# Rotary embedding from cached tables: the tables loaded into 64 partitions, with selections of 64 rows

## The chip, the cores and the metric

The kernel runs on one core of one Trainium2 chip. The metric is the time of one execution in microseconds (us). The profile's span is some 1.8 us shorter than that time, because it runs from the first to the last instruction of the program. A run that is more than 1.5% above the fastest of the same kernel counts as slow; slow runs are reported, but left out of the ratios.

## The reference

```python
# x: (8, 8, 1024, 64) float32; cos_cached, sin_cached: (1024, 32) float32
x_first, x_second = x[..., :32], x[..., 32:]
out_first  = x_first * cos_cached - x_second * sin_cached
out_second = x_first * sin_cached + x_second * cos_cached
```

Input and output are 16.8 MB each, each table is 128 KB.

## The kernel before

Eight tiles of x, 128 partitions of 16 KB each, are loaded, rotated and stored. A partition holds 64 successive positions of x, so that partition p needs the table rows of positions 64(p mod 16) to 64(p mod 16) + 63. The tables are loaded once, 8 positions to a partition, and TensorE spreads them: for each of eight blocks it multiplies the raw table by a selection matrix of zeros and ones, whose output row p picks the right raw row. A first product of the identity alone (`plus`) warms TensorE up.

```python
raw = sv[3][:, :BK]                              # 128 partitions, BK = 512
for eng, i, t in ((nc.sync, 0, sin_cached), (nc.scalar, 1, cos_cached)):
    eng.dma_start(out=raw[:, i * BK // 2:(i + 1) * BK // 2],
                  in_=t.rearrange("(q n) j -> q (n j)", q=P))
load(0, 0, F // 2); load(0, F // 2, F)           # x, all on SyncE's queue
# ... six more tiles; tile 7 in two pieces
sel = sv[3][:, BK:BK + N * P]                    # N = 2 * M = 8 selections side by side
nc.vector.tensor_copy(out=sel..., in_=plus...)   # built from the identity
nc.tensor.matmul(tp[6][:, :BK], plus, ...)       # warm-up
rt = raw.rearrange("q (t n j) -> q n t j", t=2, j=half)
for b, t in tp.items():                          # eight products in all
    for k in range(t.shape[1] // BK):
        nc.tensor.matmul(t[:, k * BK:(k + 1) * BK],
                         sel[:, (b + k) * P:(b + k + 1) * P], rt, start=True, stop=True)
# VectorE multiplies tile 0 straight from the products; ScalarE copies them to `tb` for the
# other tiles. VectorE, GpSimd and TensorE share the rest; all stores are on SyncE's queue,
# the first held back until the loads are nearly done.
```

(Before there are eight selections, in the change M = 4 that serve two products each.)

## Time and profile before

| | before |
|---|---|
| time, median (lowest to highest) | 85.07 us (85.02 to 85.08), 3 runs |
| span of the profile | 83.2 us |
| busy: VectorE, GpSimd, TensorE, ScalarE | 68.1, 65.2, 45.2, 38.1 us |
| moved by DMA | 33.8 MB, 407 GB/s over the whole span |
| last store issued / landed | 74.7 / 82.4 us |

The prediction shows the lines. PE is TensorE and PEld its weight loads, DVE is VectorE, ACT ScalarE, POOL GpSimd, SP SyncE; a q behind the name marks what the engine's queue does, such as issuing DMAs. A group in the profile reads: source line, engine, operation, output and input tile, shapes, count, then busy time, mean ns, and the idle time of the engine just before, with what ended it. An fp32 product appears as two TensorE records, which I call passes: eight products are 16 passes. The strips cut the span into 40 slices and give the busy share in tenths; PEclk is the share of TensorE's full clock that was granted, in tenths.

### The profile page before, as it was taken

The page shows a single profiled execution, that of the slowest core. Times are in us where ns is not written, and L with a number is a line of the kernel's source. Part 1 is how long each engine was busy: PE and PEld are TensorE (multiplying, and loading weights), DVE is VectorE, ACT ScalarE, POOL GpSimd, SP SyncE. Part 2 cuts the span into 40 slices and gives each one's busy share as a digit, 9 for nine tenths or more (in the row PEclk, how much of TensorE's full clock was granted, in tenths as well). Part 3 has the DMA queues.
Part 4 walks back from the last instruction along what each step waited for, and adds up shares of the span by engine and source line. Part 5 has one row for each costly group of instructions (what it writes and reads, how often), then busy time and mean ns, then how long its engine had stood idle before and what let it go on. Part 6 is the DMA issues. An engine that isn't in the chain of part 4 may idle for free.

```text
span 83.2 us, 393 instructions
## 1 busy us (share of the span) xinstructions
PE 45.2 (54%) x82; PEld 17.4 (21%) x82; DVE 68.1 (82%) x30; ACT 38.1 (46%) x34; POOL 65.2 (78%) x38
## 2 busy tenths in 40 slices
PE   3999960009971952994962948909959800000000
PEld 2244410004411401341411404204304200000000
DVE  3105999899999999999999999999999999980000
ACT  4322048954467627666449383694049290000000
POOL 3008998799999999999999999999999969920000
PEclk9999999855599999579999999996599999555555
DMA  1999999999999999989999999999999999999991
GB/s 20 346 402 445 465 402 449 433 410 457 410 465 402 418 457 402 465 377 423 428 434 465 418 410 457 402 473 402 418 465 402 457 402 473 410 410 402 420 426 44
DMA packets 3172, 33.82 MB, mean 407 GB/s; under 512 B 356, under 2 KB 612, under 8 KB 1124
## 3 DMA queue, kind: packets, MB, share of 16 engines
q1 hardware_dynamic: 3028, 33.69, 95.9%
q10 hardware_dynamic: 144, 0.13, 0.5%
HBM read 17.04 MB, written 16.78 MB: 407 GB/s over the span
## 4 chain that ended last, share of the span: by engine, by line
DVE 45%; DMA 25%; issue 12%; ACT 4%; SPq 3%; DVEq 1%
DVE w L117 40%; DMA w<-in_x_dram 25%; ACT st L124 4%; DVE st L117 3%; SPq L82 2%; DVE w L120 1%; DVEq L292 1%; SPq L77 0%; DVEq L117 0%; DVEq L120 0%
## 5 line engine op out<-in xcount | busy, mean ns | idle before, releaser
L117 DVE TENSOR_TENSOR w<-st,tb 128x3072 f32<-128x3072 f32 (+3 forms) x19 | 53.1, 2869 | 0.5 <-ACT st L124 0.5
L124 ACT COPY st<-w 128x1536 f32<-128x1536 f32 (+1 forms) x19 | 24.8, 1309 | 16.0 <-DVE w L117 16.0
L176 PE MATMUL acc<-w,plus 128*128 128x512 f32 x32 | 20.1, 714 | 19.6 <-ACT w L182 12.5
L120 POOL TENSOR_TENSOR w<-w 128x1024 f32<-128x1024 f32 (+4 forms) x12 | 25.0, 2086 | 1.9 <-DVE w L117 1.7
L121 POOL TENSOR_TENSOR w<-w 128x1024 f32<-128x1024 f32 (+4 forms) x12 | 25.0, 2085 | 0.0
L117 POOL TENSOR_TENSOR w<-w,tb 128x1280 f32<-128x1280 f32 (+1 forms) x6 | 14.2, 2368 | 5.5 <-DMA w<-in_x_dram 5.3
L176 PEld LDWEIGHTS acc<-w,plus 128*128 128x128 f32 x32 | 6.5, 224 | 31.7 <-ACT w L182 18.3
L117 DVE TENSOR_TENSOR w<-w,tab 128x2048 f32<-128x2048 f32 (+1 forms) x4 | 7.9, 2018 | 4.7 <-PE tab L227 4.7
L177 PE MATMUL acc<-w,minus 128*128 128x512 f32 x16 | 10.8, 768 | 0.0
L182 ACT COPY w<-acc 128x1024 f32<-128x1024 f32 x8 | 8.1, 1008 | 5.6 <-PE acc L177 5.6
L227 PE MATMUL tab<-w 128*128 128x512 f32 x16 | 8.2, 669 | 0.1
L177 PE MATMUL acc<-w,plus 128*128 128x512 f32 x16 | 8.2, 592 | 0.0
L235 ACT COPY tb<-tab 128x1024 f32<-128x1024 f32 (+1 forms) x5 | 4.2, 840 | 7.9 <-DVE w L117 5.0
L177 PEld LDWEIGHTS acc<-w,minus 128*128 128x128 f32 x16 | 3.8, 236 | 5.0 <-issue 5.0
L227 PEld LDWEIGHTS tab<-w 128*128 128x128 f32 x16 | 3.5, 223 | 5.6 <-issue 5.6
L177 PEld LDWEIGHTS acc<-w,plus 128*128 128x128 f32 x16 | 3.2, 199 | 4.4 <-issue 4.4
L117 DVE TENSOR_TENSOR st<-st,tb 128x1024 f32<-128x1024 f32 (+1 forms) x2 | 3.0, 1489 | 0.0
L222 PE MATMUL tab<-plus 128*128 128x512 f32 x2 | 2.1, 1140 | 1.4 <-POOL plus L100 1.4
L102 DVE COPY w<-plus 128x1024 f32<-128x1024 f32 x1 | 1.1, 1099 | 1.3 <-POOL plus L100 1.3
L105 ACT ACT_TABLE_LOAD x1 | 1.3, 1283 | 1.2 <-PEq L281 1.2
L120 DVE TENSOR_TENSOR w<-st,w 128x512 f32<-128x512 f32 (+1 forms) x2 | 1.6, 825 | 0.1
L121 DVE TENSOR_TENSOR w<-st,w 128x512 f32<-128x512 f32 (+1 forms) x2 | 1.6, 815 | 0.0
(10 smaller groups left out, 3.2 us busy)
## 6 DMA issues: line engine op xcount, KB each, us to landing
out_dram<-w SPq DMA_DIRECT2D x7, 2048.0 KB, 11.7
w<-in_x_dram SPq DMA_DIRECT2D x6, 2048.0 KB, 26.8
w<-in_x_dram SPq DMA_DIRECT2D x2, 1024.0 KB, 6.3
out_dram<-w SPq DMA_DIRECT2D x2, 768.0 KB, 7.7
w<-in_x_dram SPq DMA_DIRECT2D x1, 1280.0 KB, 34.3
w<-in_x_dram SPq DMA_DIRECT2D x1, 768.0 KB, 33.7
out_dram<-w SPq DMA_DIRECT2D x1, 512.0 KB, 7.1
w<-in_cos_cached_dram ACTq DMA_DIRECT2D x1, 128.0 KB, 2.8
```

The source lines that it names most:

```text
L82: return nc.sync.dma_start(out=xt[u][:, m0:m1], in_=xf[u][:, m0:m1])
L105: nc.scalar.mul(out=minus, in_=plus, mul=-1.0)
L117: eng.tensor_tensor(out=o, in0=a, in1=t, op=TT.mult)
L120: eng.tensor_tensor(out=o[:, :, 0], in0=c[:, :, 0], in1=s[:, :, 1], op=TT.subtract)
L121: eng.tensor_tensor(out=o[:, :, 1], in0=c[:, :, 1], in1=s[:, :, 0], op=TT.add)
L124: nc.scalar.copy(out=pt[:, :(n1 - n0) * hd], in_=xt[u][:, n0 * hd:n1 * hd])
L176: nc.tensor.matmul(a[:, k], plus, xr[:, :, k], start=True, stop=False)
L177: nc.tensor.matmul(a[:, k], plus if k else minus, sr[:, :, 1 - k], start=False, stop=True)
L182: nc.scalar.copy(out=rows(xt[u], n0, n0 + G), in_=a)
L222: nc.tensor.matmul(tp[6][:, :BK], plus, plus.unsqueeze(1).to_broadcast([P, BK // P, P]), start=True, stop=True)
L227: nc.tensor.matmul(t[:, k * BK:(k + 1) * BK], sel[:, (b + k) * P:(b + k + 1) * P], rt, start=True, stop=True)
L235: nc.scalar.copy(out=tb[:, b * BK:(b + n) * BK], in_=tp[b])
```

## The change

The intent is fewer and larger packets for the tables (2 KB rows, 64 of them, in place of 1 KB and 128) and a selection that costs half: 64 rows of four selections. Each selection serves two products, which read two halves of the raw rows.

```diff
+    Q = P // 2
-    raw = sv[3][:, :BK]
+    raw = sv[3][:Q, :2 * BK]
-        eng.dma_start(out=raw[:, i * BK // 2:(i + 1) * BK // 2],
-                      in_=t.rearrange("(q n) j -> q (n j)", q=P))
+        eng.dma_start(out=raw[:, i * BK:(i + 1) * BK],
+                      in_=t.rearrange("(q n) j -> q (n j)", q=Q))
...
+    M = N // 2
-    sel = sv[3][:, BK:BK + N * P]
+    sel = sv[3][:Q, 2 * BK:2 * BK + M * P]
-        in_=plus.rearrange("q (j k) -> q k j", k=N).unsqueeze(2).to_broadcast([P, N, N, S]))
+        in_=plus[:Q, :Q].rearrange("q (j k) -> q k j", k=M).unsqueeze(2)
+        .to_broadcast([Q, M, N, S]))
...
-    rt = raw.rearrange("q (t n j) -> q n t j", t=2, j=half)
+    rt = raw.rearrange("q (t h n j) -> q h n t j", t=2, h=2, j=half)
-                             sel[:, (b + k) * P:(b + k + 1) * P], rt,
+                             sel[:, (b + k) // 2 * P:((b + k) // 2 + 1) * P],
+                             rt[:, (b + k) % 2],
```

More of the change, by code (lines that the diff above doesn't have):

```diff
@@ L102 @@
     nc.vector.tensor_copy(
-        out=sel.rearrange("q (k r j) -> q k r j", k=N, j=S),
-        in_=plus.rearrange("q (j k) -> q k j", k=N).unsqueeze(2).to_broadcast([P, N, N, S]))
+        out=sel.rearrange("q (k r j) -> q k r j", k=M, j=S),
+        in_=plus[:Q, :Q].rearrange("q (j k) -> q k j", k=M).unsqueeze(2)
+        .to_broadcast([Q, M, N, S]))
     nc.scalar.mul(out=minus, in_=plus, mul=-1.0)
@@ L223 @@
                      start=True, stop=True)
-    rt = raw.rearrange("q (t n j) -> q n t j", t=2, j=half)
+    rt = raw.rearrange("q (t h n j) -> q h n t j", t=2, h=2, j=half)
     for b, t in tp.items():
         for k in range(t.shape[1] // BK):
-            nc.tensor.matmul(t[:, k * BK:(k + 1) * BK], sel[:, (b + k) * P:(b + k + 1) * P], rt,
-                             start=True, stop=True)
+            nc.tensor.matmul(t[:, k * BK:(k + 1) * BK], sel[:, (b + k) // 2 * P:((b + k) // 2 + 1) * P],
+                             rt[:, (b + k) % 2], start=True, stop=True)
     def first(b, n):
```

## The prediction

> **What bounds the kernel now.** I read the page's shares first, then the strips, then the queues, then the DMA issues, and last some stretches of time around the part that the change touches.
>
> ```profile
> span 83.2 us, 393 instructions
> PE 45.2 (54%) x82; PEld 17.4 (21%) x82; DVE 68.1 (82%) x30; ACT 38.1 (46%) x34; POOL 65.2 (78%) x38
> DVE  3105999899999999999999999999999999980000
> DMA  1999999999999999989999999999999999999991
> q1 hardware_dynamic: 3028, 33.69, 95.9%
> q10 hardware_dynamic: 144, 0.13, 0.5%
> ```
>
> VectorE (DVE) is the busiest engine with 68.1 us, but its strip ends four slices before the span does (a slice is 83.2/40 = 2.08 us), while the DMA strip is full from the second slice to the last but one. The two queues fill 96.4% of the time of the 16 DMA engines. The kernel moves 33.8 MB, and 33.69 MB in 0.959 x 83.2 = 79.8 us is 422 GB/s. So my reading is that the DMA engines bound it: they must start early, never run dry and be left with little extra to do. The chain of work that ended last says something else at first sight:
>
> ```profile
> DVE 45%; DMA 25%; issue 12%; ACT 4%; SPq 3%; DVEq 1%
> DVE w L117 40%; DMA w<-in_x_dram 25%; ACT st L124 4%; DVE st L117 3%; SPq L82 2%; DVE w L120 1%; DVEq L292 1%; SPq L77 0%; DVEq L117 0%; DVEq L120 0%
> ```
>
> That chain runs back from the last instruction of an engine, at 74 us, and does not contain the 8 us in which only stores drain. To see whether VectorE nonetheless holds the end, I ask how far ahead of the DMA engines the stores are issued:
>
> ```profile
> out_dram<-w SPq DMA_DIRECT2D x7, 2048.0 KB, 11.7
> out_dram<-w SPq DMA_DIRECT2D x2, 768.0 KB, 7.7
> out_dram<-w SPq DMA_DIRECT2D x1, 512.0 KB, 7.1
> w<-in_x_dram SPq DMA_DIRECT2D x2, 1024.0 KB, 6.3
> w<-in_cos_cached_dram ACTq DMA_DIRECT2D x1, 128.0 KB, 2.8
> w<-in_sin_cached_dram SPq DMA_DIRECT2D x1, 128.0 KB, 2.6
> ```
>
> A 2 MB store needs 2.10 MB / 430 GB/s = 4.9 us of its own and takes 11.7, so it stands behind some 6 us of other work and its receipt. The next view gives the slack of the last store: busy time of each engine by stretch, then the granted clock, the DMA share and the GB/s.
>
> ```profile
> 1.70:2.70 1.00, 1.00 (x2) 0.16 (x1) 0.74 (x1) 0.99 (x2) 0.00 (x0) 1.00 0.94 229
> 2.70:3.20 0.50, 0.50 (x1) 0.00 (x0) 0.00 (x0) 0.06 (x1) 0.00 (x0) 1.00 1.39 443
> 3.20:6.20 3.00, 2.85 (x5) 1.36 (x5) 0.00 (x0) 0.54 (x1) 0.00 (x0) 1.00 0.96 377
> ...
> 3.10:40.30 37.20, 24.30 (x44) 9.72 (x44) 32.85 (x13) 20.00 (x18) 32.39 (x17) 0.86 1.01 426
> ...
> 43.00:74.70 31.70, 16.50 (x32) 6.34 (x32) 31.43 (x16) 16.01 (x14) 29.42 (x14) 0.88 1.00 430
> ...
> 74.70:81.80 7.10, 0.00 (x0) 0.00 (x0) 0.00 (x0) 0.00 (x0) 0.00 (x0) 0.50 0.93 388
> ```
>
> The last store is issued at 74.7 us. After that the DMA engines still move 388 GB/s x 7.1 us = 2.75 MB, of which that store is 0.79 MB. So 1.97 MB were queued ahead of it, 4.6 us of work at 430 GB/s. VectorE could end some 4 us later, or any amount earlier, and the end would not move. The DMA share is 1.00 or 1.01 in both long stretches: there is no hole to fill. What is left to win or lose lies in the first three rows, where the tables and the first x packets go through: 229 GB/s in the first microsecond of traffic.
>
> **What the Trainium skill says.** Four places bear on it. "SBUF — State Buffer", section "Door 1: The DMA port swizzle (why [64,N] ≈ [32,N])": partitions 0 to 63 reach only 8 of the 16 ports through which DMA writes, and a 1 MiB transfer to 64 partitions measured 196 GB/s against 328 to 128. The kernel before has only 128-partition transfers, so its trace can neither confirm nor deny this. "DMA: Bandwidth & Descriptors", section "Why a DMA increments its semaphore by 16 and not by 1": a transfer whose slowest dimension is 64 is still split over 16 engines; every transfer of this trace lands in 16 parts, but those have 128 rows. The same page, section "Why small descriptors are slow (HBM only)": each packet has a fixed overhead of about 3 cycles. Here the packet records show it, somewhat larger: 1 KB takes 46 ns, 16 KB takes 611 ns, so at 26.8 bytes per ns 1 KB should be 38 ns and about 8 ns are fixed. "TensorE: Matmul & The Clock Gate", section "LDWEIGHTS (loading the stationary operand)": the time of a weight load follows the columns and not the contraction rows. All loads here have 128 rows (190 ns each once the clock is up), so no row of before tests that.
>
> **The change part by part.** Instruction order and waits are the same on every engine; I compared the two programs. Four things differ.
>
> *Packets.* Before, each table is 128 packets of 1 KB, 256 in all, 16 for each of the 16 DMA engines, 16 x 46 = 736 ns. After, it is 128 packets of 2 KB, 8 for each engine. At 8 + 2048/26.8 = 84 ns that is 8 x 84 = 672 ns: 0.06 us less for each DMA engine, and as they bound the kernel, 0.06 us off the end. Issuing 64 rows instead of 128 may take a few hundredths off the 0.38 us issue too.
>
> *Ports.* All 64 partitions lie in the half that reaches 8 ports. If two DMA engines now share one port, the tables' 262 KB go at 8 x 27 = 216 GB/s, 1.21 us in place of about 0.67: up to +0.54 us of DMA time before the x packets of each engine can follow. The first microsecond is already slow (229 GB/s, where full rate is 430)[...]; part of the sharing hides in there. Of the table phase, 1.75 to 3.11 us in the packet records, about 0.6 us is not transfer. I take half of the cost as hidden: +0.3 us, estimated, with a span of +0.1 to +0.55.
>
> *The selection copy.* VectorE's copy of the selection goes from 128x1024 (1.10 us) to 64x512, half the elements, about 0.55 us. It ends at 2.44 us now, and the first selection matmul starts at 3.58, after the tables have landed (0.74 issue + 2.6 to 2.8). So this copy waits for nobody's benefit: worth 0.
>
> *The eight products.* Sixteen passes as before, 592 ns each at full clock and about 1.1 us before it; the moving operand still has 512 columns, so I expect the same durations with 64 rows. That TensorE starts by when the tables land moves the first VectorE product (6.64 us) and all its later work by the same few tenths, well inside 4 us of slack. Worth 0.
>
> Sum: -0.06 + 0.3 with the sharing, -0.06 to -0.1 without. I give the sharing 7 chances in 10, as a measured entry of the skill says it, though for larger transfers: 0.7 x 0.26 - 0.3 x 0.08 = +0.16. I lean to the likelier branch: 85.07 + 0.18 = 85.25 us.
>
> **The rivals.** First: larger packets win and the port sharing does not show, because 262 KB are too little against the start-up latency. For it speaks that 0.6 us of the table phase is not transfer; against it that the x packets follow without a gap, so any engine time saved or lost is passed on. It would make 84.95 to 85.05. Second: the tables' landing gates the compute. For it: the first VectorE product and the first table copy wait for TensorE (4.7 and 2.9 us in the list of waits), and TensorE for the tables. If the end followed it, tables landing 0.5 us sooner or later would show in full, 84.6 or 85.6. Against it: the 4.6 us of queued stores, and the first x half lands only at 6.4 us, about when TensorE's second block is ready. Third: only 8 of the 16 DMA engines take the tables, and those end 0.6 us late in everything, because each x tile is split evenly: 85.6 to 85.7. The landing in 16 parts speaks against it. Fourth: all 16 passes slow down with 64 rows; even 50% more, some 5 us on TensorE, would come close to the slack but not over it: within 85.3.
>
> **Range and chances.** The three runs agree within 0.06 us. The branch without sharing gives 84.95 to 85.05, the one with it 85.15 to 85.6; I set 84.9 to 85.65 for 8 times in 10. A change over 2% means 1.7 us, three times the largest sum of table costs that I can work out: faster 1%, within 2% 98%, slower 1%.
>
> **What would show it.** In the profile after: a VectorE copy of about 0.55 us that nothing waits for; eight products with the old 592 ns passes; 64 packets per table; with sharing, a lower GB/s than 229 and 443 in the stretch from 1.7 to 3.2 us, table landings near 3.0 us in place of 2.6 to 2.8, the first 1 MB of x later by about 0.3 us, and the last landing later by the same. Without it, landings as before or sooner. Wrong would be: a hole in the DMA strip, the last store issued over 4 us later, or a time that moves without the first x packets moving.

## The result, and the profile after

The changed kernel takes 86.14 us (median of four runs, 85.98 to 86.52), the kernel before 85.07 us beside it (85.02 to 85.11). Ratios here are the mean time of one kernel's fast runs over the mean of the other's fast runs in the same rounds, so they are not quite the ratio of the medians. This one is 1.0132, with a 95% interval of 1.0098 to 1.0166. The kernel became slower by about 1.07 us: within 2%, but well outside the range of 84.9 to 85.65 and six times the predicted loss of 0.18 us.

The page of the changed kernel, for the lines that the prediction showed of before:

```profile
span 84.3 us, 393 instructions
PE 50.5 (60%) x82; PEld 19.0 (23%) x82; DVE 67.6 (80%) x30; ACT 38.2 (45%) x34; POOL 65.2 (77%) x38
DVE 52%; issue 18%; PE 17%; DMA 4%; ACT 2%; DVEq 1%
DVE  2002264949999999999999999999999999999600
PEclk9999999999999999985899995699999999975555
DMA  0999999999999999989999999999989788989993
```

Four things are new. The chain of work that ended last (its line stands third) now runs through TensorE for 17% of the span, where before it ran through the loads (DMA 25%). TensorE is busy 5.3 us longer with the same 82 passes. VectorE's strip has gaps in slices 4 to 9 (2 2 6 4 9 4) and now goes on until two slices before the end, where four were free. And the DMA strip has dents from slice 30 on, where it had been full. The next lines are TensorE's eight products (start, duration, line, what, what ended the idle time): first before, then after, with the group of them after below:

```profile
3.58 8.17 PE L227 MATMUL tab<-w 128*128 128x512 f32 x16
```

```profile
4.02 13.99 PE L230 MATMUL tab<-w 64*128 64x512 f32 x16 [0.58 <-DMA w<-in_cos_cached_dram]
...
L230 PE MATMUL tab<-w 64*128 64x512 f32 x16 | 14.0, 1065 | 0.6 <-DMA w<-in_cos_cached_dram 0.6
```

The same 16 passes take 13.99 us in place of 8.17, and start 0.44 us later. In the single records of before, the first passes start 0.98, 0.85 and 0.59 us apart, then the distance is 0.43 us and stays there. After, the first distance is 0.98 us and every other one is 0.85 us, to the end (a record lasts 1057 ns; records overlap). (PEclk shows the full clock in this time, in both kernels; the end of the experiments says why that misleads.) All four of VectorE's first products now wait for TensorE, 10.3 us in all against 4.7 us.

How the delay reached the end shows in the DMA issues and in the DMA share (the last but one number of each stretch; the last is GB/s):

```profile
out_dram<-w SPq DMA_DIRECT2D x7, 2048.0 KB, 7.2
out_dram<-w SPq DMA_DIRECT2D x2, 768.0 KB, 4.2
out_dram<-w SPq DMA_DIRECT2D x1, 512.0 KB, 3.6
```

```profile
60.00:72.00 12.00, 5.19 (x11) 1.69 (x10) 11.80 (x9) 5.75 (x5) 11.09 (x6) 0.93 1.01 431
```

```profile
60.00:72.00 12.00, 7.65 (x17) 2.88 (x16) 11.96 (x8) 6.49 (x7) 11.78 (x6) 1.00 0.93 396
```

The first fence shows the issues after, the second the stretch before, the third the same stretch after. A 2 MB store lands 7.2 us after its issue where it took 11.7: the queue ahead of it is almost gone. In these 12 us the DMA engines moved 396 GB/s in place of 431, 0.42 MB less, which is 0.98 us of their work. Most of it is lost in one microsecond, in which nothing moves (first before, then after):

```profile
67.00:68.00 1.00, 0.00 (x0) 0.00 (x0) 1.00 (x2) 1.00 (x2) 0.65 (x1) 1.00 1.04 442
```

```profile
67.00:68.00 1.00, 1.00 (x4) 0.40 (x3) 0.96 (x3) 0.45 (x1) 1.00 (x2) 1.00 0.01 0
```

Why just there: for each store I took how long it was issued before the store ahead of it landed, its lead. (The traces don't give the landings of the seventh and eighth store, so two leads are missing.) For the sixth store before, the fifth was issued at 56.11 us and landed 11.5 us later, at 67.6; the sixth was issued at 62.61, so its lead was 5.0 us, the smallest of all. After, the fifth landed at 61.37 + 6.5 = 67.87 and the sixth was issued only at 67.18: a lead of 0.7 us, too little to fill the queues before they ran dry.

The loads have their own, smaller part. The tables took 0.54 us to issue in place of 0.38, the first x packets started at 2.93 us in place of 2.65, and the first half tile landed at 6.80 in place of 6.42. The loads stay 0.4 us late up to the last of them (43.6 against 43.2 us). In the first stretches of traffic, for which the prediction showed 229 and 443 GB/s before, less was moved:

```profile
1.70:2.70 1.00, 1.00 (x2) 0.16 (x1) 0.26 (x1) 0.99 (x2) 0.00 (x0) 1.00 0.63 158
2.70:3.20 0.50, 0.50 (x1) 0.00 (x0) 0.00 (x0) 0.22 (x1) 0.00 (x0) 1.00 1.24 373
```

Start and hole would make 1.4 us, but the last store landed only 1.12 us later (83.47 against 82.35). Before, its 16 parts landed between 81.36 and 82.35; after, between 83.25 and 83.47. I take it that the DMA engines that were behind used the hole to catch up.

### The profile page after: what moved, and what is told of

Its sections match the earlier page's. It is cut to its first block, busy times and chain, and to the rows that moved or that the text cites. A ratio compares the mean times of both kernels' runs of the same rounds, so it can differ in the third digit from the quotient of the medians.

```text
span 84.3 us, 393 instructions
## 1 busy us (share of the span) xinstructions
PE 50.5 (60%) x82; PEld 19.0 (23%) x82; DVE 67.6 (80%) x30; ACT 38.2 (45%) x34; POOL 65.2 (77%) x38
## 4 chain that ended last, share of the span: by engine, by line
DVE 52%; issue 18%; PE 17%; DMA 4%; ACT 2%; DVEq 1%
DVE w L120 47%; PE tab L230 17%; DMA w<-in_cos_cached_dram 4%; DVE st L120 3%; ACT st L127 2%; DVE w L123 1%; DVEq L295 1%; DVE w L124 1%; DVEq L120 0%; DVEq L123 0%
## 5 line engine op out<-in xcount | busy, mean ns | idle before, releaser
L179 PE MATMUL acc<-w,plus 128*128 128x512 f32 x32 | 19.9, 709 | 17.4 <-ACT w L185 11.7
L120 DVE TENSOR_TENSOR w<-w,tab 128x2048 f32<-128x2048 f32 (+1 forms) x4 | 8.1, 2020 | 10.3 <-PE tab L230 10.3
L230 PE MATMUL tab<-w 64*128 64x512 f32 x16 | 14.0, 1065 | 0.6 <-DMA w<-in_cos_cached_dram 0.6
L230 PEld LDWEIGHTS tab<-w 64*128 64x128 f32 x16 | 5.2, 330 | 9.4 <-issue 9.4
L104 DVE COPY w<-plus 64x512 f32<-64x512 f32 x1 | 0.6, 617 | 1.3 <-POOL plus L102 1.3
## 6 DMA issues: line engine op xcount, KB each, us to landing
w<-in_x_dram SPq DMA_DIRECT2D x6, 2048.0 KB, 26.8
```

The lines of the kernel that those rows point to most:

```text
L120: eng.tensor_tensor(out=o, in0=a, in1=t, op=TT.mult)
L179: nc.tensor.matmul(a[:, k], plus, xr[:, :, k], start=True, stop=False)
L230: nc.tensor.matmul(t[:, k * BK:(k + 1) * BK], sel[:, (b + k) // 2 * P:((b + k) // 2 + 1) * P], rt[:, (b + k) % 2], start=True, stop=True)
```

## The experiments

I read the step from 0.85 to 0.43 us between passes before as TensorE's clock doubling: the Trainium skill says that it runs at half rate until activity has released it ("TensorE: Matmul & The Clock Gate", section "Part 1: The HAM clock gate"), and before shows the step some 4 us after its first pass. Theory A after reading the traces: a product with 64 active rows does not get this clock raised. The passes stay at half speed, VectorE falls behind by over 4 us, the stores lose their lead, and the DMA engines run dry for a microsecond. Its rivals were that the longer gap between the warm-up and the first selection (0.58 against 0.15 us) kept the clock down (B), that the clock follows the toggling of data (C), and that all came from the later loads (D). Before ran at 84.97 us (84.91 to 85.3, seven runs).

**e1_pad128: the change with products over 128 rows.**

```diff
+    nc.vector.memset(sv[3][64:128, :2 * BK], 0.0)
-    sel = sv[3][:Q, 2 * BK:2 * BK + M * P]
+    sel = sv[3][:128, 2 * BK:2 * BK + M * P]
-        in_=plus[:Q, :Q]...  .to_broadcast([Q, M, N, S])
+        in_=plus[:128, :Q]... .to_broadcast([128, M, N, S])    # rows 64 to 127 are zero
-    rt = raw.rearrange(...)
+    rt = sv[3][:128, :2 * BK].rearrange(...)
```

> The change as it is, but its products contract over 128 rows: rows 64 to 127 of the tables' buffer and of the selection are zero, so the result is right and the loads (64 partitions, 2 KB packets) are those of the change. Theory A (a product with 64 active rows never gets the TensorE clock raised, and the loads cost only their own few tenths): the passes fall back from 854 ns apart to 430 ns apart after the first two or three, the last store is issued near 75 us, and the time is 85.3 to 85.6, what the loads alone cost. Rival B (the clock stays low because of the 0.58 us gap between the warm-up products and the first selection, with the rows blameless): the gap is still there, so passes stay 854 ns apart and the time stays near 86.1. Rival C (the clock follows the data that toggle, not the rows): zero rows add no toggling, so as under B.

Measured: correct, 85.25 us median, fast runs 85.0 to 85.98 (a fifth at 87.01 was slow), ratio 1.0013 (0.9977 to 1.0048). TensorE's products:

```profile
3.90 8.16 PE L232 MATMUL tab<-w 128*128 128x512 f32 x16 [0.47 <-DMA w<-in_cos_cached_dram]
```

They take 8.16 us (8.17 before), although the gap of 0.47 us is there and half of the rows are zero. Rivals B and C fall, and so does D, since the loads are those of the change. The profiled run was the one at 85.98: in it one of the 16 parts of the first half tile of x landed 1.0 us after the other 15, and that part stayed about a microsecond late to the end. The other fast runs are within 85.0 to 85.25, which is a little under what I had expected.

**e2_rows64: before, with products over rows 0 to 63.**

```diff
-    nc.tensor.matmul(..., sel[:, (b + k) * P:(b + k + 1) * P], rt, ...)
+    nc.tensor.matmul(..., sel[:P // 2, (b + k) * P:(b + k + 1) * P], rt[:P // 2], ...)
```

> The kernel before with its loads untouched (128 partitions, 1 KB packets), but each of the eight products contracts over rows 0 to 63 alone; the result is wrong on purpose. Theory A: all 16 passes 854 ns apart, 14.0 us of selection passes in place of 8.2, VectorE's chain and the last store some 4 to 5 us later, and the time 85.3 to 85.9: the share of the loss that is TensorE's. Rival B (the gap): the gap is 0.15 us as before, so passes go back to 430 ns and the time is 85.07. Rival D (the whole loss comes from the later tables and x loads): 85.07 too.

Measured: the result is wrong; 85.8 us median (85.62 to 86.09), ratio 1.0091 (1.0058 to 1.0124).

```profile
3.60 13.99 PE L227 MATMUL tab<-w 64*128 64x512 f32 x16 [0.17 <-DMA w<-in_cos_cached_dram]
...
60.00:72.00 12.00, 7.40 (x16) 2.88 (x16) 11.97 (x8) 6.33 (x7) 11.77 (x5) 1.00 0.93 395
```

With the loads of before and a gap of only 0.17 us, the passes are as slow as in the change, to the hundredth. The same hole stands in the DMA share, 395 GB/s. The 64 rows alone make most of the loss.

**e3_warm: the change with four more warm-up products.**

```diff
+    for _ in range(5):
-    nc.tensor.matmul(tp[6][:, :BK], plus, ...)
+        nc.tensor.matmul(tp[6][:, :BK], plus, ...)
```

> The change, with four more warm-up products of 128 rows ahead of the selections (eight passes more), so that the clock is already raised when the 64-row passes begin. If 64 rows are slow in themselves, at any clock, the 64-row passes are 854 ns apart from the first. Theory A (64 rows only fail to raise or hold the clock): the first 64-row passes are 430 ns apart, and after some microseconds they fall back to 854 ns. Rival B: the passes are continuous here, so all 16 at 430 ns. The time is 86 to 88 in all cases, as the selections start 3 to 6 us late; the spacing of the passes decides.

Measured: correct, 85.89 us median (85.76 to 86.03), ratio 1.0098 (1.0071 to 1.0125).

```profile
7.54 7.13 PE L231 MATMUL tab<-w 64*128 64x512 f32 x16
...
60.00:72.00 12.00, 6.70 (x15) 2.41 (x14) 11.97 (x8) 6.59 (x6) 11.51 (x6) 1.00 1.01 434
```

Once the clock is up, 64-row passes run 0.43 us apart (only the second came 0.53 us after the first), and they do not fall back. That part of my expectation was wrong: 64 rows did not raise the clock in the change and in e2_rows64, but they hold it for the 7 us seen here. The second line shows no hole: the smallest lead of a store was 3.3 us. Why is the time 0.9 us up all the same? The spans of its four runs are 83.3 to 83.6 us, those of before mostly 83.2 (83.1 to 83.5), so inside the program only 0.1 to 0.4 us were lost; the rest lies outside it. This kernel has 16 more instructions on TensorE than the change (weight loads and passes), and in this trace alone of the first six the packet records show a late 8 KB packet on the instruction queue, at 85.8 us. That this packet is the 0.6 us is my inference and was not tested.

**e4_mid: as e1_pad128, with the tables in partitions 32 to 95.** (The port map that the expectation names is that of "SBUF — State Buffer", section "Door 1", as in the prediction.)

```diff
-    raw = sv[3][0:64, :2 * BK]          # as in e1_pad128
+    raw = sv[3][32:96, :2 * BK]
+    nc.vector.memset(sv[3][0:32, :2 * BK], 0.0)
+    nc.vector.memset(sv[3][96:128, :2 * BK], 0.0)
-        in_=plus[:128, 0:64]...
+        in_=plus[:128, 32:96]...
```

> As the first of these (128-row products with zero rows), but the tables go to partitions 32 to 95, which lie in both halves of the port map of the Trainium skill, so that 64 rows reach all 16 ports. If shared ports are what the loads of the change cost, x lands 0.3 to 0.4 us sooner than with partitions 0 to 63 and the time is 85.0 to 85.1. If the cost is the issue of such a load (0.54 us in place of 0.38) or the later first packet, the time is that of the first run, 85.3 to 85.6.

Measured: correct, 85.61 us median, fast runs 85.43 to 85.74 (a fourth at 87.2 was slow), ratio 1.0058 (1.0027 to 1.0089). x did not land sooner: 6.68 us in this trace, between the 6.61 of e1_pad128 (15 of its 16 parts) and the 6.80 of the change, both with partitions 0 to 63. The tables took 0.59 and 0.60 us to issue, and sine's first packet started only at 2.93 us. So reaching the other ports bought nothing that could be seen, but as the issue became longer too, the run does not exclude a small share of the ports. The products took 9.81 us: here the clock rose only after six slow passes. The gap of 0.68 us need not be the reason: e7_issue had four slow passes with a gap of 0.21 us, where before had two with 0.15. What sets their number is open.

In the second call, before took 85.07 us (84.64 to 85.26, 11 runs).

**e5_first128: 128 rows for the first four products, 64 for the rest.**

```diff
     # on top of e1_pad128
+    K_ = P if b + k < 4 else Q
-    nc.tensor.matmul(..., sel[:, ...], rt[:, (b + k) % 2], ...)
+    nc.tensor.matmul(..., sel[:K_, ...], rt[:K_, (b + k) % 2], ...)
```

> The change, but only the first four of its eight products contract over 128 rows (zero rows as before), the last four over 64; the result is right and no instruction is added to TensorE. Theory A as the runs so far leave it (64 rows can't raise the clock but hold it once raised): the clock rises during the first four products and all passes of the last four are 430 ns apart; no hole in the DMA strip; 85.0 to 85.3. If holding in the warm-up run was due to its extra warm-up products, the last eight passes fall back to 854 ns and the last store slips by some 3 us, still without a hole.

Measured: correct, 85.29 us median (85.09 to 85.57, six runs), ratio 1.0026 (1.0007 to 1.0044).

```profile
L233 PE MATMUL tab<-w 128*128 128x512 f32 x8 | 6.4, 979 | 0.8 <-DMA w<-in_cos_cached_dram 0.8
L233 PE MATMUL tab<-w 64*128 64x512 f32 x8 | 3.7, 602 | 0.0
...
60.00:72.00 12.00, 6.05 (x14) 2.20 (x12) 11.97 (x8) 6.01 (x6) 11.51 (x6) 0.97 1.01 430
```

The last line, the stretch from 60 to 72 us, shows no hole. The 64-row passes are now the fast ones, at a mean of 602 ns against 1065 in the change. So the first four products are warm-up enough, though these 64-row passes last only 3.7 us; that 64 rows hold the clock rests on the 7 us of e3_warm, since TensorE's clock stays up for as long as 5 us when it is idle (e7_issue, from 12.7 to 17.7 us). With TensorE mended the time is still 0.1 to 0.4% up. In e1_pad128 and e6_pad96, with the same loads, the difference is not clear of noise.

**e6_pad96: as e1_pad128, with 96 rows.** The edit is that of e1_pad128 with 96 in place of 128.

> As the first run, with 96 rows in place of 128 (rows 64 to 95 zero). If the clock follows the share of active rows with a limit near the full array, it stays low: passes 854 ns apart, about 86. If half of the array is merely the wrong side of the limit, it rises as with 128 rows and the time is 85.0 to 85.3. I lean to the second.

Measured: correct, 85.18 us median (85.02 to 85.62), ratio 1.0021 (0.9995 to 1.0047).

```profile
4.02 9.93 PE L232 MATMUL tab<-w 96*128 96x512 f32 x16 [0.59 <-DMA w<-in_cos_cached_dram]
```

The start and the gap are those of the change to 0.01 us, and the last 32 rows hold zeros, yet the clock rises (after six slow passes). With the change this is the cleanest pair for the row count: 13.99 us with 64 rows, 9.93 us with 96, and the start and the gap equal.

**e7_issue: the issue of a table load by itself.**

```diff
-    row = const.tile([1, 2 * hd], fp32, name="row")
-    for i in range(2):
-        nc.sync.dma_start(out=row[:, i * hd:(i + 1) * hd], in_=xf[i][0:1, 0:hd])
+    row = const.tile([P, BK], fp32, name="row")
+    nc.sync.dma_start(out=row[:64, :],        in_=<cosine, 64 rows of 2 KB>)
+    nc.sync.dma_start(out=row[:, :BK // 2],   in_=<cosine, 128 rows of 1 KB>)
```

> The kernel before, whose two small pacing loads of x rows (0.30 and 0.23 us to issue, when the queue is quiet) become one load of a table into 64 partitions of 2 KB and one into 128 partitions of 1 KB. If the shape sets the issue time, the first takes about 0.16 us longer than the second, as 0.54 against 0.38 at the start of the kernels; if the longer issue at the start comes from something else there, both take the same. Either way 256 KB more pass the DMA engines: 85.5 to 85.8.

Measured: correct, one run at 87.99 us, its state unknown.

```profile
13.68 0.52 SPq L93 DMA_DIRECT2D row<-in_cos_cached_dram  x1
43.91 0.34 SPq L94 DMA_DIRECT2D row<-in_cos_cached_dram  x1
```

The second column is the time to issue: 0.52 us for 64 rows of 2 KB, 0.34 for 128 rows of 1 KB. The difference of 0.18 us is near that of the kernels' starts (0.54 and 0.38). The two loads were issued 30 us apart, the first behind other loads and the second not, so this run alone does not show that the shape sets it; but in all ten traces a table load at the start took 0.54 to 0.60 us with 64 rows and 0.38 to 0.39 with 128. The time missed my expectation by over 2 us, through a flaw of mine: the second load overwrites the first one's tile and waited for it until 43.91 us, and the stores behind it on the same queue came 4.1 us late (the first at 44.43, before at 40.29). Between 43 and 46 us the DMA share fell to 0.39 in place of 1.02. That is a hole again, made in another way, and again it reached the end.

**e8_nowarm: before without its warm-up product.**

```diff
-    nc.tensor.matmul(tp[6][:, :BK], plus, ..., start=True, stop=True)
```

> The kernel before without its one warm-up product (loads and 128-row selections unchanged). Theory: the clock rises one window of 3.4 us later than with it, up to seven more passes at 854 ns, the last store 2 to 3 us later; the stores are still issued 2 us or more before the one ahead of them has landed, so the DMA strip has no hole and the time is 85.0 to 85.1. If the lead of the stores isn't what decides, and the lateness of TensorE passes through, it is over 85.6.

Measured: correct, 85.13 us median (85.08 to 85.24), ratio 1.0009 (0.9987 to 1.003). The products took 9.74 us, with six slow passes in place of two, and the last store was issued at 75.97 us, 1.3 us later; I had expected 2 to 3. The clock rose at 9.0 us in place of 5.7, 3.2 us later by the unrounded records. Between two changes of the clock the records of all ten traces show multiples of 3.41 us, the 3.4 us of the expectation. The smallest lead of a store was 4.3 us. A late TensorE alone cost nothing here that stands clear of noise, as the lead lasted.

Smallest lead and DMA rate from 60 to 72 us, side by side (leads from the issues and landings of each trace):

| kernel | smallest lead, us | GB/s | ratio |
|---|---|---|---|
| before | 5.0 | 431 | 1 |
| e5_first128 | 3.7 | 430 | 1.0026 |
| e3_warm | 3.3 | 434 | 1.0098 (0.6 us of it outside the span) |
| e2_rows64 | 1.1 | 395 | 1.0091 |
| the change | 0.7 | 396 | 1.0132 |

The clock records in the traces show the clock itself. Here is when each trace first records the full clock, in us from the start of the span:

| kernel | full clock from, us | what TensorE does then |
|---|---|---|
| e3_warm, before, e1_pad128 | 4.8, 5.7, 6.0 | the distance of its passes falls to 0.43 us |
| e7_issue, e8_nowarm | 7.5, 9.0 | the same |
| e4_mid, e6_pad96, e5_first128 | 9.6, 9.7, 9.8 | the same |
| e2_rows64, the change | 26.2, 27.0 | its 64-row passes are over since 17.6 and 18.0; its next products, over 128 rows, began at 23.3 and 23.7 |

PEclk counts the time before the first record as full, which is why its strip shows 9 in the first 17 slices of the change, while the passes there are 854 ns apart. For the same reason a late first record raises the mean granted clock of a run. It is 0.89 to 0.92 in all four runs of the change and all four of e2_rows64, and 0.82 to 0.87 in every run of the other kernels, which speaks against the profiled runs being exceptions.

Together the parts fit: 1.0091 for the rows alone times about 1.002 for the loads alone (1.0013, 1.0026 and 1.0021 in the three runs with fast or nearly fast products) is 1.011, inside the interval of the change. No run beat the kernel before beyond its scatter, and nothing here points to one that would: DMA work bounds both, and the larger packets save it only 0.06 us (8 of 84 ns in place of 16 of 46 for each DMA engine).

## Why the prediction was wrong

- **What bounds the kernel** was right: the DMA engines, which must not run dry. The loss beyond the start is a hole in their strip.
- **Packets**: right in size, 84 ns for 2 KB in the packet records. The saving is too small to be seen.
- **Ports**: the estimate of +0.3 us was near the late landing of x (+0.4 us in the profiled run; 0.1 to 0.2 us in the times of the mended kernels), but for a reason that no run supports. The table packets took 84 ns at the median on one queue and 89 on the other, where a shared port would make it some 150 (an estimate, from half of the prediction's 26.8 bytes per ns), and partitions of both halves were no better. What the runs show is a longer issue, 0.16 to 0.18 us for each such load, and a later first packet. I had guessed that the issue would become shorter. The prediction's signs of sharing therefore don't decide: two came true, a lower rate in the first stretches (158 and 373 GB/s) and x later by about 0.4 us, but loads that merely start later show both as well.
- **The selection copy**: right, 617 ns in place of 1099, and nothing waited for it.
- **The eight products**: this is the step that failed. "The moving operand still has 512 columns, so I expect the same durations with 64 rows" looked at the columns alone and took it for granted that the clock would rise. The durations at each clock are the same (a record of 1057 ns against 1057 to 1061 at the slow one, 589 against 592 at the fast one); but with 64 rows the clock did not rise during these products, so the passes came 854 ns apart instead of 430, and the sum went from 8.17 to 13.99 us. "Worth 0" was a loss of 0.9% by itself (e2_rows64). What the prediction cites on weight loads ("TensorE: Matmul & The Clock Gate", section "LDWEIGHTS (loading the stationary operand)"), that their time does not follow the rows, holds here: 187 ns with 64 rows in e3_warm, 190 ns with 128 before.
- **The slack** that should have caught it was read at one place only. I worked out 4.6 us for the last store; the sixth had a lead of 5.0 us, and of that lead some 2 us must remain, since with 0.7 and 1.1 us the DMA ran dry for about a microsecond, the fifth store's 1.7 us in the change already cost a little (366 GB/s from 61 to 64 us, 426 before), and 2.2 us and more cost nothing (432 GB/s from 43 to 60 us in the change and in e2_rows64, as before). So about 3 us were to be had, and the sixth store came 4.57 us later. Two of the prediction's three signs of being wrong came true: a hole in the DMA strip, and the last store issued over 4 us later (79.31 against 74.69 us).
- **The fourth rival** named the mechanism and dismissed it with a wrong sum: it called 50% more on the passes "some 5 us". The passes before filled about 8 us; what happened was 71% more of that, 5.8 us, and it did not stay "close to the slack but not over it".
- **Slips that change nothing**: the weighted sum takes 0.26 for the branch with sharing, where -0.06 + 0.3 is 0.24; and not every transfer before has 128 rows, as the two small pacing loads have one.

## What to carry to other kernels

When a change alters the shape of TensorE's operands, ask not only what a pass costs at full clock, but whether the clock will still rise: here padding with zero rows to 96 or 128, or giving only the first products more rows, recovered nearly all of the loss. When lateness is said to be hidden, measure the lead of every transfer over the one ahead of it and take the smallest, less what a transfer needs to start. And look at single passes in order of time: a mean and a busy share hide whether a burst ran slow from end to end.

## What the Trainium skill lacked or had wrong

- "TensorE: Matmul & The Clock Gate", on the release of the clock by how busy TensorE is: nothing on active rows. Here 14 us of unbroken 64-row fp32 passes never got it raised (the change and e2_rows64), 96 and 128 rows did, zero rows included, and 64 rows held it once raised (7 us in e3_warm). Where between 64 and 96 the limit lies, whether the rows of the weights or those of the moving operand count, and whether other types behave so, is open.
- "SBUF — State Buffer", on the halved rate for partitions 0 to 63: not seen with two loads of 128 KB (84 ns per 2 KB packet, and no gain from partitions 32 to 95). The runs do not reach the 1 MiB at which the page measured it, so they do not refute it.
- "DMA: Bandwidth & Descriptors": I found no issue time by shape there; it was 0.52 to 0.60 us for 64 rows of 2 KB, 0.34 to 0.39 for 128 rows of 1 KB.
